# Transposing transfers of the SwiGLU product: issued by SyncE instead of ScalarE, later in SyncE's order, merged later, and in the second feed-forward only

## The chip, the cores and the metric

The kernel runs on one core of one Trainium2 chip. The metric is the device time of one execution in microseconds (us); a comparison takes the median of several runs. The core has these engines, by the names that the profile uses: PE (TensorE, matmuls and transposes through the array), DVE (VectorE), ACT (ScalarE), POOL (GpSimd) and SP (SyncE, which here only issues transfers). Transfers are carried out by 16 DMA engines; SP and ACT each have a queue of their own to them (q1 and q10 in the profile).

## The reference

One decoder layer on 256 positions of width 2048, in float32: a feed-forward, a pair of token mixers (retention and sliding-window attention) and a second feed-forward, each behind an RMS norm that is scaled and shifted by a conditioning vector, and a final norm. The change is in the feed-forwards:

```
def swiglu(h, w_gu, w_down):
    gate, up = jnp.split(h @ w_gu, 2, axis=-1)
    return (jax.nn.silu(gate) * up) @ w_down

x = x + 0.5 * mod[:, 2] * swiglu(h, w_ffn1_gu, w_ffn1_down)   # the first
...
x = x + 0.5 * mod[:, 8] * swiglu(h, w_ffn2_gu, w_ffn2_down)   # the second
return rms_norm(x, norm_final)
```

The inner width is 5632. The conditioning values mod are products of silu(c) with a weight matrix of 18432 rows.

## The kernel before

**Matmuls.** The 256 positions are two token tiles of 128. Every product is worked out in two parts for precision: weights and activations are each split into a high part (rounded to fp32r) and a low part, and three matmuls are made for each piece (L327 high x high, L328 low activation x high weight, L329 high activation x low weight). Weights come in tiles of 512 rows by 512 columns, 1 MB, into `raw`, a ring of four buffers (RAWS = 4) (`load`, L310). `split` (L331) makes of each half tile (256 rows) a high part wh by a cast on ACT (L335) and a low part wl by a subtraction on DVE (L336); each has a ring of three buffers. A half tile feeds 12 matmuls. A raw buffer is free for the next load when wl of its second half is done. `gemm` (L384) does one column block of 512: four tiles in the feed-forward's first product, with two PSUM banks of a ring of four.

**A feed-forward.** The inner width is 11 column blocks (ci = 0 to 10). For each, `ffn_up` (L585) makes the gate's product and the up product (8 weight tiles), and `swiglu_up` (L559) makes silu(gate) on ACT (L572) and times up on DVE (L573), for each token tile, into a tile s of 128 x 512 floats. The second product contracts over the inner width, so s is needed turned, inner width on the partitions. There are two ways to turn it:

- `transpose_to` (L413): four PE transposes of 128 x 128 (L417) into a PSUM bank and one copy back to SBUF (L418). The first six blocks of the first feed-forward, which are made in another loop (the groups of its beginning), and the last block of both use it.
- `turn_by_dma` (L424): transposing transfers move 2-byte words, so a float is taken apart. The function `apart` copies the low and the high words into two planes on ACT (L432) and issues a transposing transfer for each plane on ACT's queue (L433); `together` merges the two turned planes into the destination (L439), on an engine that is left open (`nc.any`, ACT or DVE). It has two buffers (tag "a"), one for each token tile of a block.

Blocks 6 to 9 of the first feed-forward and 0 to 9 of the second go the second way: 14 blocks, 28 tiles, 56 transfers.

**What sets the order.** SP's instructions stand in the order of the program. Those of PE, DVE and ACT are put in an order, at build time, by a planner that runs the program on a model of the chip and takes what the model says can start; on the chip each engine then takes its instructions strictly in that order. Within the program, `gemm` calls `step` (L300) after each weight tile, which advances the next piece of waiting side work by one. `later` (L549) is the side work of a block: `apart` of the two token tiles is called in the second and third step of the block behind, `together` in the fifth and sixth. Beside all this, `conditioning` (L241) loads rows of the conditioning weights (L199) and sums them on DVE (L204), at a set pace; in the second feed-forward these rows take buffers of the same ring `raw`, one after about every fifth weight tile.

## Time and profile before

| what | value |
|---|---|
| median of 3 runs | 2452.04 us |
| the runs | 2444.63, 2452.04, 2461.02 us |
| the profiled execution, its time | 2453.29 us |
| its span (first to last instruction) | 2451.4 us |
| TensorE clock granted in it, mean | 0.996 |
| transfers that transpose | 56, on ACT's queue |
| second feed-forward, its column blocks, in the span | about 1737 to 2203 us |

The profile is of one execution. Times in its rows are in us unless marked ns. A row of the waits gives the waiting engine and line, who ended the wait, the total, the number and the longest. A row of the stretches gives, for each engine, its busy time and in brackets the number of its instructions, then the granted clock of PE, the mean busy share of the 16 DMA engines and what they moved. A row of the timeline gives start, length, engine, line, operation, destination and sources, and in square brackets how long the engine was idle before and what ended that. Matmuls overlap in the records: one lasts 0.39 us there, but in a row of them one starts every 0.23. ACTq and SPq are the engines' issuing of transfers. A few per cent of matmul records can be missing.

### The profile page before, as it was taken

Reading aid. Unit: us, or ns where it says so; the run is one execution under the profiler, and the core shown is the slowest. Engines: PE = TensorE matmul, PEld = TensorE weight load, DVE = VectorE, ACT = ScalarE, POOL = GpSimd, SP = SyncE. Lnnn points to the kernel's source line nnn. Section 1 sums busy time; section 2 is a strip of 40 time slices with the busy share of each in tenths; the row PEclk is TensorE's granted clock in tenths of the full one; section 3 lists DMA queues with packets and bytes.
Section 4 is the critical chain, followed back from the end, with each engine's and each line's share of the span. In section 5 each row is a group of like instructions: output and inputs, shape, how many; then the busy total and the mean of one; then the engine's idle time right before and its main releaser. Section 6 shows DMA issues by size and latency. Waiting matters only on the chain. (4 is left out here: it accounts for less than half of the span.)

```text
span 2451.4 us, 29087 instructions
## 1 busy us (share of the span) xinstructions
PE 2393.8 (98%) x10798; PEld 1950.0 (80%) x10798; DVE 1711.5 (70%) x2767; ACT 1216.2 (50%) x1664; POOL 5.6 (0%) x14
## 2 busy tenths in 40 slices
PE   6999999999999999999999999999999999999998
PEld 4778888788787777788888888887788788888886
DVE  6998777678877677886666776767655556555656
ACT  6544544454445455554444444455544444444544
POOL 0000000000000000000000000000000000000000
PEclk9999999999999999999999999999999999999999
DMA  9897689998775655566677777754777667765563
GB/s 349 335 336 276 225 313 328 292 324 318 294 266 197 234 206 212 206 213 219 234 267 247 252 256 267 276 189 172 230 237 242 219 239 246 260 219 192 188 200 121
DMA packets 274545, 606.43 MB, mean 247 GB/s; under 512 B 40097, under 2 KB 40481, under 8 KB 255585
## 3 DMA queue, kind: packets, MB, share of 16 engines
q1 hardware_dynamic: 242434, 590.56, 68.0%
q10 hardware_dynamic: 31040, 8.40, 2.3%
q0 software_dynamic: 928, 5.61, 0.6%
q8 instruction: 85, 1.39, 0.2%
q14 instruction: 58, 0.48, 0.1%
HBM read 595.06 MB, written 2.12 MB: 244 GB/s over the span
## 5 line engine op out<-in xcount | busy, mean ns | idle before, releaser
L336 DVE TENSOR_TENSOR wl<-raw,wh 128x1024 fp32r<-128x1024 f32 (+1 forms) x828 | 994.1, 1206 | 580.7 <-ACT wh L335 577.3
L335 ACT CAST wh<-raw 128x1024 fp32r<-128x1024 f32 (+1 forms) x828 | 860.1, 1040 | 992.6 <-PE pa L328 952.2
L327 PE MATMUL pa<-wh,hh 128*128 128x512 f32 x2224 | 872.5, 393 | 8.6 <-ACT wh L335 8.0
L328 PE MATMUL pa<-wh,hl 128*128 128x512 f32 x2224 | 871.3, 392 | 2.3 <-DVE hl L500 1.8
L329 PE MATMUL pa<-wl,hh 128*128 128x512 f32 x2224 | 801.3, 393 | 11.3 <-DVE wl L336 11.0
L329 PEld LDWEIGHTS pa<-wl,hh 128*128 128x128 f32 x2224 | 416.5, 189 | 106.1 <-DVE wl L336 20.0
L327 PEld LDWEIGHTS pa<-wh,hh 128*128 128x128 f32 x2224 | 418.9, 189 | 100.1 <-ACT wh L335 10.6
L328 PEld LDWEIGHTS pa<-wh,hl 128*128 128x128 f32 x2224 | 419.1, 188 | 90.4 <-DVE hl L500 2.5
L328 PE MATMUL pa<-wh,a 128*128 128x512 f32 x992 | 384.4, 390 | 0.0
L327 PE MATMUL pa<-wh,a 128*128 128x512 f32 x992 | 367.7, 390 | 1.3 <-DVE t L543 1.2
L329 PE MATMUL pa<-wl,a 128*128 128x512 f32 x992 | 367.7, 391 | 0.8 <-DVE wl L336 0.8
L327 PEld LDWEIGHTS pa<-wh,a 128*128 128x128 f32 x992 | 186.6, 188 | 41.3 <-DVE t L543 1.9
L329 PEld LDWEIGHTS pa<-wl,a 128*128 128x128 f32 x992 | 186.4, 188 | 40.5 <-DVE wl L336 2.2
L328 PEld LDWEIGHTS pa<-wh,a 128*128 128x128 f32 x992 | 186.5, 188 | 38.6
L204 DVE CUSTOM_DVE_ANT_0 slot<-slot,cact 128x512 f32<-128x512 f32 (+1 forms) x252 | 192.9, 812 | 9.4 <-DMA slot<-in_w_ada_dram 9.2
L204 DVE CUSTOM_DVE_ANT_0 raw<-raw,cact 128x512 f32<-128x512 f32 (+1 forms) x260 | 166.9, 694 | 38.2 <-DMA raw<-in_w_ada_dram 27.6
L368 DVE TENSOR_TENSOR a<-slot,a 128x512 fp32r<-128x512 f32 x124 | 84.8, 684 | 14.8 <-ACT a L367 14.8
L367 ACT CAST a<-slot 128x512 fp32r<-128x512 f32 x124 | 76.6, 618 | 15.1 <-PE pa L329 14.7
L204 DVE DVE_READ_ACCUMULATOR2_ANT sums<- 128x1 f32 x512 | 41.7, 81 | 0.0
L418 ACT COPY slot<-ps 128x512 f32<-128x512 f32 x52 | 29.5, 584 | 23.7 <-PE ps L417 23.5
L459 ACT ACTIVATE pd<-x_sb 128x512 f32<-128x512 f32 x32 | 19.0, 593 | 35.2 <-DVE x_sb L544 32.5
L439 ACT COPY slot<-a 128x512 uint16<-128x512 uint16 x22 | 16.5, 770 | 39.2 <-DMA a<-a 39.1
(164 smaller groups left out, 1037.0 us busy)
## 6 DMA issues: line engine op xcount, KB each, us to landing
raw<-in_w_ffn_gu_dram SPq DMA_DIRECT2D x152, 1024.0 KB, 5.1
raw<-in_w_in_dram SPq DMA_DIRECT2D x104, 1024.0 KB, 5.0
raw<-in_w_ffn_down_dram SPq DMA_DIRECT2D x88, 1024.0 KB, 5.1
slot<-in_w_ada_dram SPq DMA_DIRECT2D x76, 1024.0 KB, 7.3
raw<-in_w_ada_dram SPq DMA_DIRECT2D x64, 1024.0 KB, 4.8
raw<-in_w_ffn_gu_dram SPq DMA_DIRECT2D x24, 768.0 KB, 6.5
raw<-in_w_swa_branch_dram SPq DMA_DIRECT2D x16, 1024.0 KB, 5.0
raw<-in_w_ret_branch_dram SPq DMA_DIRECT2D x16, 1024.0 KB, 5.1
```

Source lines behind the costliest of these rows:

```text
L204: nc.vector.tensor_tensor_reduce(out=w[:, at], in0=w[:, at], in1=cact[:, at], scale=1.0, scalar=0.0, op0=ALU.mult, op1=ALU.add, accum_out= ...
L327: nc.tensor.matmul(ps, ah[:, j, ts], wh[:, j, :], start=first, stop=False)
L328: nc.tensor.matmul(ps, al[:, j, ts], wh[:, j, :], start=False, stop=False)
L329: nc.tensor.matmul(ps, ah[:, j, ts], wl[:, j, :], start=False, stop=last)
L335: nc.scalar.copy(hi, src)
L336: nc.vector.tensor_sub(lo, src, hi.bitcast(F32))
L367: nc.scalar.copy(hi, v)
L368: nc.vector.tensor_sub(lo, v, hi.bitcast(F32))
L418: nc.any.tensor_copy(dest, ps[:, : n * P])
L439: nc.any.tensor_copy(into[:, :, :, i], turned[:, i])
L459: nc.scalar.activation(side_bank(), src, AF.Square, accum_out=dest)
```

## The change

Three things change in the code.

- Taking apart and issuing are separated. `apart` only makes the two word copies on ACT; a new function `turn` issues the two transposing transfers, on SP's queue instead of ACT's. Since SP keeps the program's order, the place where `turn` is called is its place among the weight loads.
- `later` has a new schedule: the word copies in the second and third step, as before; `turn` of the two token tiles in the seventh and eighth; the merging copies of both tiles in the step behind these, the first of the next block but one.
- `ffn_up` gets the set of column blocks that go by transfer. The call of the first feed-forward gives none, so its blocks 6 to 9 are turned by PE; the call of the second gives blocks 0 to 9, as before.

```
-                nc.scalar.dma_start_transpose(turned[:, i], planes[:, i, :])
+
+        def turn():
+            for i in range(2):
+                nc.sync.dma_start_transpose(turned[:, i], planes[:, i, :])
...
-        return apart, together
+        return apart, turn, together
...
     def later(work):
 
-        for first, _ in work:
+        (a0, t0, m0), (a1, t1, m1) = work
+        for f in (a0, a1, None, None, None, t0, t1, m0):
             yield
-            first()
-        yield
-        for _, second in work:
-            yield
-            second()
+            if f is not None:
+                f()
+        m1()
...
-    def ffn_up(held, w, tiles, first, bg=None):
+    def ffn_up(held, w, tiles, first, bg=None, turned=()):
...
-            swiglu_up(bg, bu, tiles, ci, by_dma=ci < DFF // CH - 1)
+            swiglu_up(bg, bu, tiles, ci, by_dma=ci in turned)
...
-    ffn_up(held, w_ffn2_gu[0], tiles, 0, head)
+    ffn_up(held, w_ffn2_gu[0], tiles, 0, head, range(DFF // CH - 1))
```

In the changed file the lines are a few further down: the transfers are L436, the merging copies L442, silu is L574.

The order on SP, in the second feed-forward, from the load of the last gate tile of column block 1 to the first gate tile of block 2. raw is the ring of weight tiles, a_2421 and a_2423 are the buffers in which the two token tiles of column block 0 are turned. Before:

```order
L312 DMA raw_2441_13692<-in_w_ffn2_gu_dram 128x4x512
L312 DMA raw_2448_13729<-in_w_ffn2_gu_dram 128x4x512
L199 DMA raw_2453_13763<-in_w_ada_dram 128x2048
L312 DMA raw_2454_13768<-in_w_ffn2_gu_dram 128x4x512
L312 DMA raw_2459_13805<-in_w_ffn2_gu_dram 128x4x512
L312 DMA raw_2464_13839<-in_w_ffn2_gu_dram 128x4x512
L312 DMA raw_2475_13884<-in_w_ffn2_gu_dram 128x4x512
```

The same place after the change:

```order
L312 DMA raw_2441_13680<-in_w_ffn2_gu_dram 128x4x512
L312 DMA raw_2448_13717<-in_w_ffn2_gu_dram 128x4x512
L199 DMA raw_2453_13751<-in_w_ada_dram 128x2048
L312 DMA raw_2454_13754<-in_w_ffn2_gu_dram 128x4x512
L312 DMA raw_2459_13789<-in_w_ffn2_gu_dram 128x4x512
L436 DMA_TRANSPOSE a_2421_13565<-a_2421_13565 128x4x128 x2
L312 DMA raw_2464_13825<-in_w_ffn2_gu_dram 128x4x512
L436 DMA_TRANSPOSE a_2423_13569<-a_2423_13569 128x4x128 x2
L312 DMA raw_2475_13872<-in_w_ffn2_gu_dram 128x4x512
```

Four transfers have come in, a pair behind each of two loads. The load raw_2459 goes into the buffer of raw_2441, four back in the ring, and raw_2464 into that of raw_2448.

The order on ACT at the turning of the same column block 0. wh is the high part of a half weight tile, t the tile s, slot the destination. Before, from the word copies to the merges (the other two merges of this block are on DVE):

```order
L432 COPY a_2421_13573<-t_2420_13570 128x512 x2
L432 COPY a_2423_13577<-t_2422_13574 128x512 x2
L433 DMA_TRANSPOSE a_2421_13573<-a_2421_13573 128x4x128
L335 CAST wh_2434_13633<-raw_2431_13615 128x1024
L433 DMA_TRANSPOSE a_2421_13573<-a_2421_13573 128x4x128
L433 DMA_TRANSPOSE a_2423_13577<-a_2423_13577 128x4x128
L335 CAST wh_2437_13655<-raw_2436_13653 128x1024
L433 DMA_TRANSPOSE a_2423_13577<-a_2423_13577 128x4x128
L335 CAST wh_2439_13672<-raw_2436_13653 128x1024
L439 COPY slot_2392_13421<-a_2423_13577 128x4x128
```

After the change the word copies stand at the same place, and the rest of this moves behind the cast wh_2449:

```order
L335 CAST wh_2444_13699<-raw_2441_13680 128x1024
L335 CAST wh_2449_13719<-raw_2448_13717 128x1024
L442 COPY slot_2392_13413<-a_2421_13565 128x4x128 x2
L335 CAST wh_2451_13735<-raw_2448_13717 128x1024
L574 ACTIVATE t_2469_13862<-pa_2424_13570 128x512
L335 CAST wh_2455_13756<-raw_2454_13754 128x1024
L574 ACTIVATE t_2471_13866<-pa_2425_13571 128x512
L442 COPY slot_2392_13413<-a_2423_13569 128x4x128 x2
L335 CAST wh_2457_13772<-raw_2454_13754 128x1024
```

The merges of a_2421 stand one cast behind the cast wh_2444, with whose half tile the buffer of raw_2441 comes free; those of a_2423 one cast (wh_2455) behind wh_2451, with which that of raw_2448 comes free. All four are on ACT here.

The order on ACT at column block 1, whose buffers are a_2470 and a_2472. On SP its first pair of transfers stands behind a load into the buffer of raw_2491, its second behind one into that of raw_2498. Before, around the word copies and the merge that is on ACT:

```order
L432 COPY a_2470_13877<-t_2469_13874 128x512 x2
L432 COPY a_2472_13881<-t_2471_13878 128x512 x2
L433 DMA_TRANSPOSE a_2470_13877<-a_2470_13877 128x4x128
L335 CAST wh_2483_13937<-raw_2480_13919 128x1024
L433 DMA_TRANSPOSE a_2470_13877<-a_2470_13877 128x4x128
L433 DMA_TRANSPOSE a_2472_13881<-a_2472_13881 128x4x128
L335 CAST wh_2487_13962<-raw_2486_13960 128x1024
L433 DMA_TRANSPOSE a_2472_13881<-a_2472_13881 128x4x128
L335 CAST wh_2489_13978<-raw_2486_13960 128x1024
L439 COPY slot_2392_13421<-a_2472_13881 128x4x128
```

After:

```order
L335 CAST wh_2494_14005<-raw_2491_13987 128x1024
L335 CAST wh_2499_14025<-raw_2498_14023 128x1024
L335 CAST wh_2501_14042<-raw_2498_14023 128x1024
L442 COPY slot_2392_13413<-a_2470_13865 128x4x128 x2
L574 ACTIVATE t_2519_14169<-pa_2473_13870 128x512
L335 CAST wh_2504_14060<-raw_2503_14058 128x1024
L574 ACTIVATE t_2521_14173<-pa_2474_13871 128x512
L335 CAST wh_2506_14077<-raw_2503_14058 128x1024
L442 COPY slot_2392_13413<-a_2472_13869 128x4x128 x2
L335 CAST wh_2509_14095<-raw_2508_14093 128x1024
```

Here the merges stand two casts behind the cast with whose half tile the buffer comes free (wh_2494 and wh_2501), not one. Counted in the same way over the ten blocks, it is one cast at blocks 0 and 5 for both token tiles and at 2 and 7 for the first, and two or more at the others.

## The prediction, made blind

> **What bounds the kernel now.** I read the page first: the share of each engine, the waits, the DMA queues.
>
> ```profile
> span 2451.4 us, 29087 instructions
> PE 2393.8 (98%) x10798; PEld 1950.0 (80%) x10798; DVE 1711.5 (70%) x2767; ACT 1216.2 (50%) x1664; POOL 5.6 (0%) x14
> q1 hardware_dynamic: 242434, 590.56, 68.0%
> q10 hardware_dynamic: 31040, 8.40, 2.3%
> ACT slot L439 <- DMA a<-a: 39.1, 17, 4.7
> DVE slot L439 <- DMA a<-a: 28.6, 13, 5.0
> ```
>
> TensorE (PE) is the bound: 98% busy. So an edit on ACT, DVE or SP is worth only the PE time that it frees or costs. The last two rows (the waits) name what this change touches: the merging copies (L439) stand waiting for a transposing transfer 30 times, 67.7 us in all. What matters is how much of that reaches PE. For this I took stretches of 20 us around each place where PE stood still beside a transfer, and two undisturbed ones (400 and 2000):
>
> ```profile
> core 0: us, PE busy (x) PEld busy (x) DVE busy (x) ACT busy (x) POOL busy (x), PEclk, DMA share, GB/s
> 360.00:380.00 20.00, 18.67 (x83) 15.14 (x82) 14.61 (x31) 9.81 (x12) 0.00 (x0) 1.00 0.91 299
> 460.00:480.00 20.00, 15.22 (x57) 11.11 (x57) 10.11 (x21) 8.97 (x11) 0.00 (x0) 0.91 0.89 227
> 400.00:420.00 20.00, 20.00 (x89) 16.54 (x89) 16.16 (x30) 10.39 (x13) 0.00 (x0) 1.00 0.99 324
> 1758.00:1778.00 20.00, 18.44 (x82) 14.92 (x81) 11.49 (x18) 8.35 (x9) 0.00 (x0) 1.00 0.82 230
> 1850.00:1870.00 20.00, 19.51 (x85) 15.50 (x85) 11.14 (x12) 8.92 (x11) 0.00 (x0) 1.00 0.77 269
> 1937.00:1957.00 20.00, 16.26 (x61) 12.92 (x61) 6.75 (x8) 7.70 (x8) 0.00 (x0) 0.83 0.76 184
> 2026.00:2046.00 20.00, 19.53 (x87) 15.85 (x86) 9.73 (x12) 9.06 (x11) 0.00 (x0) 1.00 0.79 221
> 2000.00:2020.00 20.00, 20.00 (x90) 16.57 (x89) 10.52 (x14) 8.84 (x10) 0.00 (x0) 1.00 0.52 178
> ```
>
> An undisturbed stretch holds 89.5 matmuls, 0.2235 us each. Those missing elsewhere, times this: first feed-forward 6.5 and 32.5, so 1.5 + 7.3 = 8.8 us; second 7.5, 4.5, 28.5 and 2.5, so 1.7 + 1.0 + 6.4 + 0.6 = 9.7 us. Everything that the transposing transfers cost PE is 18.5 us, 0.75% of the span. That caps the gain.
>
> The timeline of the costliest stop in the second feed-forward shows how it comes about:
>
> ```profile
> 1936.01 1.29 ACTq L433 DMA_TRANSPOSE a<-a  x1
> ...
> 1942.03 0.39 PE L328 MATMUL pa<-wh,hl 128*128 128x512 f32 x1
> 1944.54 0.45 DVE L439 COPY slot<-a 128x512 uint16<-128x512 uint16 x1 [4.40 <-DMA a<-a]
> 1944.89 3.48 DVE L336 TENSOR_TENSOR wl<-raw,wh 128x1024 fp32r<-128x1024 f32 x3
> ...
> 1946.16 1.22 PE L329 MATMUL pa<-wl,hh 128*128 128x512 f32 x2 [3.74 <-DVE wl L336]
> 1947.18 0.63 PE L327 MATMUL pa<-wh,hh 128*128 128x512 f32 x1
> 1947.61 0.63 PE L328 MATMUL pa<-wh,hl 128*128 128x512 f32 x1
> ...
> 1951.83 0.40 PE L327 MATMUL pa<-wh,hh 128*128 128x512 f32 x1
> 1952.06 0.39 PE L328 MATMUL pa<-wh,hl 128*128 128x512 f32 x1
> ```
>
> DVE sits in front of a merging copy, behind which the low part of the weights (wl) is queued; PE wants wl and stands 3.74 us. Afterwards its matmuls start 0.43 us apart instead of 0.23 for some 5 us. Of the 6.4 us, 3.9 are the stop (1942.03 to 1946.16, less one matmul) and 2.5 the slow restart. The 1.56 us idle of the 1758 row left the clock (PEclk) at 1.00, the 3.74 here took it to 0.83.
>
> **The change, part by part.**
>
> *First feed-forward: four column blocks go back to PE transposes.* Gone: 16 transfers with their copies, hence the stops of 8.8 us. Added: 8 transposes in each block. Priced by the last block, which does this already, in the chain of waits:
>
> ```profile
> 2203.62 0.87 PE ps L417 x8
> ```
>
> 4 x 0.87 = 3.5 us, all on PE. Their evacuations (two copies a block) replace eight word copies a block, off the path. A wait of PE for the product that it transposes would cost extra; that last block shows none, I take 0, at most 1 us a block. Net -5.3 us (-5.3 to -1.3).
>
> *Second feed-forward: ACT loses 40 issues, SP gains them.* It frees up to 4 x 1.25 us of ACT a block, at a place where its casts wait for PE anyway (1.67 us before each, rows below): 0, since PE is never waiting for ACT there. On SP four issues of about 1.2 us a block (1.21 to 1.29 in the rows quoted) stand ahead of weight loads. A load has three weight tiles of 5.44 us each (two halves of 2.72, below) before it is wanted, 16.3 us, and lands in 5.1 us (row below), so 2.5 us per pair is covered; without that cover each pair would cost up to 2.5 us of PE. The transfers wait for ACT's word copies, with the weight loads queued behind; these copies stand eight casts, some 21 us, ahead of the merges, so SP doesn't wait: 0. The later merges hold the two buffers of `turn_by_dma` longer; the next word copies come 13 casts behind: 0. POOL's queue is not touched.
>
> *Where the merges now stand.* The code calls them at the ninth step, but ACT and DVE are ordered by the planner, and it pulls them forward, right behind the issues. The cadence of one half tile, in rows of the timeline (the last one is the SP queue's, its later loads merged into it):
>
> ```profile
> 1925.00 1.05 ACT L335 CAST wh<-raw 128x1024 fp32r<-128x1024 f32 x1 [1.67 <-PE pa L328]
> 1927.72 1.05 ACT L335 CAST wh<-raw 128x1024 fp32r<-128x1024 f32 x1 [1.67 <-PE pa L328]
> 1927.75 0.39 PE L327 MATMUL pa<-wh,hh 128*128 128x512 f32 x1
> 1928.65 0.62 PE L329 MATMUL pa<-wl,hh 128*128 128x512 f32 x2
> 1928.81 1.23 DVE L336 TENSOR_TENSOR wl<-raw,wh 128x1024 fp32r<-128x1024 f32 x1 [1.50 <-ACT wh L335]
> 1930.06 17.57 SPq L312 DMA_DIRECT2D raw<-in_w_ffn_gu_dram  x4
> ```
>
> A cast every 2.72 us; its wl is done 2.32 us after it starts; SP's next load leaves at 2.34. There are three wh buffers, so a cast runs two halves ahead of its matmuls, which want wl 0.9 us after they start: a cast may be 2 x 2.72 + 0.9 - 2.34 = 4.0 us late before PE stops.
>
> Column block 0, with C the start of the cast wh_2444 (the rows of ACT and SP are in the section on the change). SP passes the load raw_2459 when raw_2441 is free: T = C + 2.34. Directly behind it the first tile's two transfers. ACT has one cast in between (wh_2449) and is at the merges at C + 3.77. When do the transfers land? Two transfers of before left within 0.3 us behind a load (rows of the SP and ACT timelines: the load, the transfer, the merge that waited for it):
>
> ```profile
> 1804.17 0.37 SPq L312 DMA_DIRECT2D raw<-in_w_ffn_gu_dram  x1
> 1804.44 1.20 ACTq L433 DMA_TRANSPOSE a<-a  x1
> 1810.34 0.77 ACT L439 COPY slot<-a 128x512 uint16<-128x512 uint16 x1 [2.31 <-DMA a<-a]
> 2160.74 0.37 SPq L312 DMA_DIRECT2D raw<-in_w_ffn_gu_dram  x1
> 2160.95 1.21 ACTq L433 DMA_TRANSPOSE a<-a  x1
> 2166.39 0.77 ACT L439 COPY slot<-a 128x512 uint16<-128x512 uint16 x1 [1.80 <-DMA a<-a]
> raw<-in_w_ffn_gu_dram SPq DMA_DIRECT2D x152, 1024.0 KB, 5.1
> ```
>
> 6.2 and 5.65 us after the load's issue: 5.9. From below, the load itself (5.1) bounds it. The second plane comes behind the first: q10's 2.3% of 2451.4 us over 56 transfers is 1.0 us each; the 0.45 us between DVE's landing at 1944.54 and ACT's next merge is less; I take 0.7. So T + 5.9 and T + 6.6, that is C + 8.24 and C + 8.94. A pair of merges ends 0.76 after the second landing (one takes 0.77): C + 9.7. The next cast was due at C + 5.44: 4.26 late, 0.26 past the slack. From it hangs everything of the second tile: wl ends and the load raw_2464 leaves at C + 12.04, the transfers land at C + 17.94 and 18.64, their merges end at C + 19.4. Only one cast stands ahead of them, the next (wh_2457) was due at C + 10.88 + 0.26: 8.26 late, 4.26 past the slack. A stop of about 4.3 us, plus the slow restart of 2.5, plus the 0.26: 7.0 us.
>
> In the changed order this place (one cast between release and merge, for both tiles) comes twice among the ten blocks, at 0 and 5, since the conditioning loads shift the ring of four; blocks 2 and 7 have it for the first tile, and their second tile's transfers leave right behind the first's, with a load between, so they land a few us later, when ACT is one cast further; I reckon one more cast's length past the slack, 0.26 + 1.05 = 1.3 us. The other six have two casts between: ACT arrives 2.72 us later, the cast behind is then 1.5 us late, inside the slack: 0. Sum 2 x 7.0 + 2 x 1.3 = 16.6 us against 9.7 now: +6.9.
>
> From below: landing at T + 5.1 and 5.5 makes the same steps end with the second cast 6.8 late, a stop of 2.8, between the 1.56 us idle that cost no restart and the 3.74 that did; I count none: 2 x 2.8 = 5.6 us, -4.1 against now (with restarts +0.9). From above: the longer landing, T + 6.2, and the second plane a whole issue (1.3 us) behind: stops of 1.2 + 5.2 and the restart, 8.9 twice, and 2 twice: 21.8 us, +12.1.
>
> [...]
>
> Sum: -5.3 + 6.9 = +1.6 us. The profiled execution took 2453.3 us (span 2451.4), the median of the three runs is 2452.0, so it stands 1.3 above; the sum against it gives 2454.9, on the median 2453.6. I say 2453.
>
> **The rivals.** About 1% (24.5 us) is what a measurement of this kernel can tell from no change.
>
> The spread of all 56 landings:
>
> ```profile
> DMA to landing us min/median/max: 2.4/4.9/20.9
> ```
>
> - *Transfers land with the load.* [...] For it: the fastest landing, 2.4 us, shows that a transfer by itself is short. Against: the two landings of 5.65 and 6.2.
> - *The first feed-forward doesn't gain.* Its stop at 462 may come from loads that are late there anyway (DMA share 0.89 to 0.99 in its rows, against 0.52 at 2000); then only 1.5 us go, 3.5 come: +2.0 + 6.9 = +8.9, 2461. Against: merging copies stood for up to 5.0 us (the waits above), more than the 4.0 us of slack worked out above, which is enough for such a stop.
> - *SP's queue is slow, and the kernel slower.* If SP's transfers land 3 us later than reckoned (T + 9), the steps above give 14 us at each of blocks 0 and 5 (stops of 3.4 and 7.4, a restart or two), about 6 at 2 and 7, and 1 at the other six: 46 us, +36 against now, +31 in all: 2483. It passes 1% from about T + 8.5. For it: landings reach 20.9 us. Against: the DMA engines have room in the second feed-forward, share 0.52 to 0.82 in its stretches.
> - *The late merging that the code writes is not what runs.* That is part of the forecast already: the planner undoes it.
>
> **How the numbers follow.** Forecast 0.58 (2443 to 2463 by its bounds: -5.3 - 4.1 to -1.3 + 12.1), landing with the load 0.22, no gain in the first feed-forward 0.10, slow queue 0.08, something unseen 0.02. The range 2440 to 2468 takes the first three, with a few microseconds for runs that lay from 2444.6 to 2461.0. Faster by over 1% would need more than the 18.5 us there are: 0.03, for what I don't see. Slower by over 1% is the slow queue and a bit: 0.09. Within 1%: 0.88.
>
> **What would show it.** The stops of 360 and 460 gone, and 32 more transposes in the L417 group on t. In the second feed-forward, ACT's waits in front of merges longer than now (about 4.5 us each at blocks 0, 2, 5, 7, about 1.7 elsewhere), a stop of about 4 us with a slow restart at each of blocks 0 and 5, none as long elsewhere. Wrong if landings of SP's transfers are not 5.5 to 7 us behind their load, if weight loads come late for casts, or if PE stops at the new transposes.

## The result, and the profile after the change

The changed kernel takes 2435.14 us (median of 6 runs, 2434.28 to 2438.25), the kernel before beside it 2454.68 us (6 runs, 2444.63 to 2465.43): a ratio of 0.9922, 95% interval 0.9893 to 0.9951. On another chip it was 2435.93 against 2457.70 us, 0.9911 (0.9887 to 0.9935). So it is some 20 us, 0.8%, faster. That is inside the 1% that was forecast, but 5 us below the low end of the range, and on the other side of "before" than the sum of terms said (+1.6 us). The runs also lie closer together: 4 us apart, where those of before are 21 us apart.

The page of the changed kernel, its lines that answer to those shown of before:

```profile
span 2433.4 us, 29081 instructions
PE 2390.0 (98%) x10830; PEld 1949.4 (80%) x10830; DVE 1701.0 (70%) x2735; ACT 1222.5 (50%) x1672; POOL 5.7 (0%) x14
q1 hardware_dynamic: 264194, 595.81, 69.8%
q10 hardware_dynamic: 576, 1.05, 0.1%
```

The profiled execution took 2435.17 us, and its span is 18.0 us shorter than that of before. PE has 32 more instructions (the transposes of four blocks) and yet is busy for 3.8 us less; its idle time, span less busy, fell from 57.6 to 43.4 us. The transfers have moved from q10 to q1: q10 has 7.35 MB less, 131 KB for each of the 56, which is 128 x 512 words of two bytes. The waits in front of the merging copies:

```profile
ACT slot L442 <- DMA a<-a: 28.7, 16, 3.5
...
DVE slot L442 <- DMA a<-a: 1.5, 2, 0.7
```

ACT and DVE still stand there 18 times for 30.2 us, the longest for 3.5 (before: 30 times, 67.7 us, 5.0). What came of it on PE is in the stretches, taken around the longest stops of before, at the first one of the second feed-forward (1757) and once where there was none (2000):

```profile
core 0: us, PE busy (x) PEld busy (x) DVE busy (x) ACT busy (x) POOL busy (x), PEclk, DMA share, GB/s
459.00:479.00 20.00, 20.00 (x90) 16.58 (x89) 15.25 (x28) 9.34 (x10) 0.00 (x0) 1.00 0.95 364
...
1757.00:1777.00 20.00, 20.00 (x90) 16.57 (x89) 10.43 (x15) 11.72 (x14) 0.00 (x0) 1.00 0.88 288
1935.00:1955.00 20.00, 20.00 (x90) 16.57 (x89) 11.98 (x16) 10.77 (x13) 0.00 (x0) 1.00 0.86 239
2000.00:2020.00 20.00, 20.00 (x90) 16.58 (x89) 13.16 (x18) 9.41 (x12) 0.00 (x0) 1.00 0.65 227
```

Every one is full: 90 matmuls, clock 1.00. In the whole of the second feed-forward the waits of PE have no row any more; from 340 to 620 us one of 0.3 us is left. Before, they were these (first the stretch of the first feed-forward's last blocks, 340 to 620 us, then the second feed-forward, 1737 to 2203 us):

```profile
PE pa L327 <- ACT wh L335: 4.7, 2, 3.2
PE pa L329 <- DVE wl L336: 1.3, 1, 1.3
...
PE pa L329 <- DVE wl L336: 5.8, 3, 3.7
PE pa L327 <- ACT wh L335: 0.4, 1, 0.4
```

Of the 18.0 us, the prediction's own count of the stops (18.5 with their restarts) less 3.5 us of transposes gives 15.0. The starts of the same matmuls in the two traces say 14.6: 4.5 from 340 to 620 us, 10.1 in the second feed-forward. The rest lies at places without a transfer, mostly from 20 to 40 and 650 to 670 us, which differ between executions of before as well.

### Column block 0 of the second feed-forward, where the prediction expected a stop of 4.3 us

The timeline of the changed kernel, rows of SP, ACT and DVE (the conditioning's sums are L204):

```profile
1756.52 2.82 SPq L312 DMA_DIRECT2D raw<-in_w_ffn_gu_dram  x2
...
1758.24 0.69 DVE L204 CUSTOM_DVE_ANT_0 raw<-raw,cact 128x512 f32<-128x512 f32 x1
1758.86 0.08 DVE L204 DVE_READ_ACCUMULATOR2_ANT sums<- 128x1 f32 x1
...
1759.39 2.61 SPq L436 DMA_TRANSPOSE a<-a  x2
1759.62 1.06 ACT L335 CAST wh<-raw 128x1024 fp32r<-128x1024 f32 x1 [1.66 <-PE pa L328]
1760.71 1.23 DVE L336 TENSOR_TENSOR wl<-raw,wh 128x1024 fp32r<-128x1024 f32 x1 [0.63 <-ACT wh L335]
1762.10 0.53 SPq L312 DMA_DIRECT2D raw<-in_w_ffn_gu_dram  x1
1762.34 1.06 ACT L335 CAST wh<-raw 128x1024 fp32r<-128x1024 f32 x1 [1.66 <-PE pa L328]
...
1764.78 1.40 ACT L442 COPY slot<-a 128x512 uint16<-128x512 uint16 x2 [1.39 <-DMA a<-a]
1766.05 1.04 ACT L335 CAST wh<-raw 128x1024 fp32r<-128x1024 f32 x1
...
1769.25 1.40 ACT L442 COPY slot<-a 128x512 uint16<-128x512 uint16 x2
```

The cast wh_2444 is the one at 1759.62: that is C. The load raw_2459 is the second of the two in the first row; that row ends at 1759.34 and an issue takes 0.37, so it left at 1758.97. That is C - 0.65, where the prediction had T = C + 2.34. It left 0.03 us after the last sum on the conditioning row (1758.86 + 0.08) and 3 us before wl of raw_2441 was done (1760.71 + 1.23 = 1761.94). So it went into the buffer of the conditioning row, not of raw_2441, as the section on the change said. The buffer of raw_2441 is then left for the load after it (raw_2464), which left at 1762.10. The ring of four doesn't turn strictly: a conditioning row gives its buffer back early, and the next load takes it.

The rest of the first tile's step came as reckoned. The transfers landed at 1764.76, 5.8 us behind the load's issue (T + 5.9 was said); two merges took 1.27; the next cast started at 1766.05, 1.0 us late instead of 4.3, and no stop followed. The second tile, from which the prediction's stop of 4.3 us came, was early too: its load left at C + 2.5 instead of C + 12.0, and its merges (1769.25) did not wait at all.

Not every block is like this one. The time from issue to landing, over the 40 transfers of the changed kernel:

```profile
DMA to landing us min/median/max: 4.4/5.5/9.1
```

The first tile's transfers landed 5.8 to 6.4 us behind the load (or the conditioning row) ahead of them at eight of the ten blocks, but 8.7 and 9.5 us behind it at blocks 2 and 7, where two other loads had left within 3.5 us before; four second tiles were over 7 us as well. That is outside the 5.5 to 7 us that the prediction named. No stop came of it: at blocks 2 and 7 three casts start between the load and the merge, not two as at the other eight, and ACT waited for 1.9 and 2.8 us.

### The profile page after: what moved, and what is told of

It reads as the page before. It is cut to its first block, busy times and chain, and to the rows that moved or that the text cites. A ratio compares the mean times of both kernels' runs of the same rounds, so it can differ in the third digit from the quotient of the medians.

```text
span 2433.4 us, 29081 instructions
## 1 busy us (share of the span) xinstructions
PE 2390.0 (98%) x10830; PEld 1949.4 (80%) x10830; DVE 1701.0 (70%) x2735; ACT 1222.5 (50%) x1672; POOL 5.7 (0%) x14
## 3 DMA queue, kind: packets, MB, share of 16 engines
q8 instruction: 85, 1.39, 0.2%
## 5 line engine op out<-in xcount | busy, mean ns | idle before, releaser
L327 PE MATMUL pa<-wh,hh 128*128 128x512 f32 x2224 | 870.3, 393 | 3.4 <-ACT wh L335 2.9
L328 PE MATMUL pa<-wh,hl 128*128 128x512 f32 x2224 | 870.1, 391 | 2.2 <-DVE hl L503 1.7
L329 PE MATMUL pa<-wl,hh 128*128 128x512 f32 x2224 | 798.9, 392 | 4.0 <-DVE wl L336 3.9
L327 PEld LDWEIGHTS pa<-wh,hh 128*128 128x128 f32 x2224 | 418.0, 188 | 93.4 <-ACT wh L335 4.3
L329 PEld LDWEIGHTS pa<-wl,hh 128*128 128x128 f32 x2224 | 415.5, 188 | 95.7 <-DVE wl L336 9.8
L328 PEld LDWEIGHTS pa<-wh,hl 128*128 128x128 f32 x2224 | 418.3, 188 | 89.4 <-DVE hl L503 2.4
L328 PE MATMUL pa<-wh,a 128*128 128x512 f32 x992 | 383.8, 389 | 0.0
L329 PE MATMUL pa<-wl,a 128*128 128x512 f32 x992 | 367.6, 390 | 1.4 <-DVE wl L336 1.4
L327 PE MATMUL pa<-wh,a 128*128 128x512 f32 x992 | 367.2, 390 | 0.3 <-DVE t L546 0.2
L329 PEld LDWEIGHTS pa<-wl,a 128*128 128x128 f32 x992 | 185.6, 188 | 42.4 <-DVE wl L336 4.5
L327 PEld LDWEIGHTS pa<-wh,a 128*128 128x128 f32 x992 | 186.1, 188 | 40.6 <-DVE t L546 0.9
L328 PEld LDWEIGHTS pa<-wh,a 128*128 128x128 f32 x992 | 186.2, 188 | 38.5
L204 DVE CUSTOM_DVE_ANT_0 slot<-slot,cact 128x512 f32<-128x512 f32 (+1 forms) x252 | 192.9, 815 | 23.9 <-DMA slot<-in_w_ada_dram 23.8
L204 DVE CUSTOM_DVE_ANT_0 raw<-raw,cact 128x512 f32<-128x512 f32 (+1 forms) x260 | 167.1, 696 | 38.5 <-DMA raw<-in_w_ada_dram 28.0
L204 DVE DVE_READ_ACCUMULATOR2_ANT sums<- 128x1 f32 x512 | 42.7, 83 | 0.0
L442 ACT COPY slot<-a 128x512 uint16<-128x512 uint16 x38 | 26.8, 769 | 28.8 <-DMA a<-a 28.7
```

The source lines that it names most:

```text
L204: nc.vector.tensor_tensor_reduce(out=w[:, at], in0=w[:, at], in1=cact[:, at], scale=1.0, scalar=0.0, op0=ALU.mult, op1=ALU.add, accum_out= ...
L327: nc.tensor.matmul(ps, ah[:, j, ts], wh[:, j, :], start=first, stop=False)
L328: nc.tensor.matmul(ps, al[:, j, ts], wh[:, j, :], start=False, stop=False)
L329: nc.tensor.matmul(ps, ah[:, j, ts], wl[:, j, :], start=False, stop=last)
L442: nc.any.tensor_copy(into[:, :, :, i], turned[:, i])
```

## The experiments

The times are medians in us:

| run | first feed-forward, blocks 6 to 9 | second, blocks 0 to 9 | time (range) | ratio to before on the same chip |
|---|---|---|---|---|
| before | ACT's queue, early | ACT's queue, early | 2454.7 to 2463.2 on five occasions | 1 |
| the change | PE | SP, late | 2435.14 (2434.28 to 2438.25) | 0.9922 |
| the change again | PE | SP, late | 2435.93 (2435.37 to 2436.37) | 0.9911 |
| first only | PE | ACT's queue, early | 2440.66 (2439.49 to 2441.86) | 0.9930 (0.9914 to 0.9946) |
| second only | ACT's queue, early | SP, late | 2450.74 (2442.43 to 2452.36) | 0.9968 (0.9952 to 0.9985) |
| no transfers | PE | PE | 2445.43 (2443.99 to 2445.86) | 0.9948 (0.9929 to 0.9967) |
| both by SP | SP, late | SP, late | 2431.79 (2431.47 to 2432.05) | 0.9893 (0.9878 to 0.9909) |
| SP early | PE | SP, early | 2440.62 (2439.76 to 2442.07) | 0.9930 (0.9914 to 0.9946) |
| both SP early | SP, early | SP, early | 2449.85 (2447.39 to 2451.22) | 0.9956 (0.9940 to 0.9973) |
| one step later | PE | SP, one load later | 2434.98 (2434.61 to 2436.86) | 0.9909 (0.9885 to 0.9933) |
| rows early | PE | SP, late | 2436.06 (2434.86 to 2437.05) | 0.9913 (0.9883 to 0.9942) |
| late on ACT | ACT's queue, late | ACT's queue, late | 2438.12 (2436.82 to 2452.32) | 0.9930 (0.9905 to 0.9954) |

"First only", "both by SP", "SP early" and "no transfers" ran on one chip; "the change again", "second only", "one step later" and "rows early" on another; "both SP early" and "late on ACT" on one more each. The ratio takes in all runs of both kernels, so it is not exactly the quotient of the two medians. Where two versions from different chips are compared below, a difference of a microsecond says little: the change itself was 2435.1 on one and 2435.9 on the other.

### The parts of the change, one at a time

The change again, as the base on the second chip:

> The changed kernel itself, on the same chip as the three others. Both theories: 2434 to 2439 us, runs within some 4 us of each other; it is the base of the comparisons.

2435.93 us, runs 1 us apart.

First only: the schedule and the queue of before, without the blocks of the first feed-forward.

```
-            swiglu_up(bg, bu, tiles, ci, by_dma=ci < DFF // CH - 1)
+            swiglu_up(bg, bu, tiles, ci, by_dma=ci in turned)
...
-    ffn_up(held, w_ffn2_gu[0], tiles, 0, head)
+    ffn_up(held, w_ffn2_gu[0], tiles, 0, head, range(DFF // CH - 1))
```

> The kernel before with one part of the change alone: the first feed-forward turned by PE, the second left as it was (transfers on ACT's queue, merges where they were). Theory A, the two halves add up: the stops of the first feed-forward (8.8 us) go and 3.5 us of PE transposes come, the second keeps its stops (9.7 us in the profile of before, more or less in another run): 5 us faster than before, and the spread from run to run of before, some 20 us, stays for the most part. Rival B, the first feed-forward is all there is: the whole 19 us, with the small spread of the changed kernel. Rival C, the stops there come from late loads and stay: 2 us slower.

17.8 us faster than before: not theory A's 5, nearly B's 19. In the second feed-forward one stop is left, here in the waits of PE from 1730 to 2196 us:

```profile
PE pa L329 <- DVE wl L336: 2.9, 1, 2.9
```

So not all of the 17.8 us belongs to the first feed-forward. By the starts of the matmuls this trace is 3.4 us shorter than the first trace of before from 340 to 620 us, and 5.4 us shorter in the second feed-forward, where it has one wait of PE in place of four although the code is that of before, and the order of ACT's and DVE's work too. Its merges wait for their transfers for less there (29.7 us in all, against 47.2); why is open.

Second only: the other half, the first feed-forward as before.

```
+        if not late:
+            for f in (lambda: a0(True), lambda: a1(True), None, m0, m1):
...
-    ffn_up(held, gu, tiles, EARLY)
+    ffn_up(held, gu, tiles, EARLY, None, range(DFF // CH - 1))
+    late.append(1)
```

> The second feed-forward as after the change, blocks 6 to 9 of the first as before it (issued by ACT in the second and third step, merged in the fifth and sixth). Theory A, both halves of the change bring something: the second feed-forward has no stops at its transfers, the first has those of before (9.0 us in the one trace) and not the 3.5 us of transposes, so after + 5.5 us, 2441, and more (up to 2455) if these stops are longer in other runs than in the traced one; and the runs lie as far apart as those of before (some 10 to 20 us), since it is these stops that vary. Rival B, the gain belongs to the first feed-forward alone: no faster than before, 2452 to 2460. Rival C, the gain belongs to the second alone: 2432, after - 3.5, runs close together.

2450.74 us, 14.8 above the change again on the same chip and 7.0 below before, with runs 10 us apart: theory A. B would have been before's time, C a time below the change's. Its waits of PE from 340 to 620 us (L330 and L328 are L329 and L327 here):

```profile
PE pa L330 <- DVE wl L337: 4.5, 1, 4.5
PE pa L328 <- ACT wh L336: 4.0, 1, 4.0
```

This is one of its shorter executions (2444.36 us). In the second feed-forward it has no wait of PE, as after the change. This run and the change again differ in the first feed-forward alone, so its part is worth 14.8 us of the median, and the second's the 7.0 that are left to before. Taken the other way round, by "first only", it is 17.8 and some 5, but there part of the second feed-forward's gain is in the 17.8.

Two more traced executions of the kernel before are to show what makes its runs differ.

> The kernel before, one more execution with its trace, to see what differs between its executions (2444 to 2465 us so far). Theory A: the stops at the transposing transfers of the first feed-forward differ, in place and size (9.0 us in the first trace), everything else is the same within a microsecond or two. Rival B: the second feed-forward's stops differ. Rival C: the difference is spread over the whole span.

> As the look before, another execution: the span less that of the first trace (2451.4 us) should be the difference of the stops of 340 to 520 us by theory A, of those of 1737 to 2203 us by B.

The spans were 2446.6 and 2456.3 us, against 2451.4 in the first trace. The waits of PE from 340 to 620 us in the longest of the three:

```profile
PE pa L327 <- ACT wh L335: 5.7, 3, 2.7
PE pa L329 <- DVE wl L336: 4.6, 1, 4.6
```

That is 10.3 us against 6.0 in the first trace (and 5.6 in the shortest), while the second feed-forward had 6.6, 6.2 and 6.1 us. So theory A holds for the longest: by the starts of the matmuls it is 8.0 us behind the first trace from 340 to 620 us (4.3 of them are these waits; it also has three slow restarts there against one, the granted clock at 0.91, 0.91 and 0.83 in 366 to 386, 466 to 486 and 418 to 428 us), and 3.1 us ahead of it elsewhere, which makes the 4.9. The 4.8 us between the first and the shortest are not there; they are spread over the beginning, the place around 660 us and the second feed-forward, 1.2 to 1.8 us in each.

No transfers: what PE's transposes cost.

```
-    ffn_up(held, w_ffn2_gu[0], tiles, 0, head, range(DFF // CH - 1))
+    ffn_up(held, w_ffn2_gu[0], tiles, 0, head)
```

> No transposing transfers at all: both feed-forwards turned by PE. Against the changed kernel ten more blocks of 8 transposes at 0.87 us come on PE: 8.7 us slower than the changed kernel if that has no stops left in the second feed-forward, as its profile says. If PE also had to wait for the products that it turns, more. If the changed kernel still loses something to its transfers that the profile does not show, less.

9.5 to 10.3 us above the change: ten blocks at 0.87 us are 8.7, and by the starts of the matmuls the second feed-forward is 9.1 longer, 0.91 a block. So the transfers of the changed kernel cost PE nothing that can be seen, and the price of the transposes is nearly right.

Both by SP: the first feed-forward's blocks by SP as well.

```
-    ffn_up(held, gu, tiles, EARLY)
+    ffn_up(held, gu, tiles, EARLY, None, range(DFF // CH - 1))
```

> The changed kernel with the transfers of SP, at the new places, in the first feed-forward as well (blocks 6 to 9), so without its PE transposes. Theory A, what stops PE is a merge that stands too soon behind a transfer of ACT's queue: the stops are gone here too and the 3.5 us of PE transposes with them, 3.5 us faster than the changed kernel. Rival D, the first feed-forward keeps the DMA engines busy (share 0.89 to 0.99), transfers land late whoever issues them: stops of 5 to 10 us come back there, 2 to 7 us slower than the changed kernel.

3.3 to 4.1 us below the change, about the 3.5 of the transposes, on another chip but with ranges that don't touch: the fastest version here, 1.07% below before. Its first feed-forward has no transposes on PE and no stops; by the starts of the matmuls it is 9.1 us shorter there than the first trace of before, where the prediction had counted 8.8 us of stops.

### Why the merges don't wait for long

Two runs bring back the prediction's T. In the first the transfers leave one load later and the merges are called right behind them:

```
-        for f in (a0, a1, None, None, None, t0, t1, m0):
+        for f in (a0, a1, None, None, None, None, t0, t1):
...
+        m0()
         m1()
```

> After the change, but the transfers one step (one weight load) later on SP, and the merging copies called right behind them. At column block 0 the first pair then leaves behind the load into the buffer of raw_2441, that is at C + 2.5, as the prediction had it for the change itself. Theory A, the planner knows when the load leaves and moves the merges with it, so that ACT waits only for what a transfer takes longer on the chip than the planner reckons (1 to 3.5 us now), inside the 4.0 us of slack: no stop, as after within 2 us. Rival B, the prediction's step (a merge stands so and so many casts behind the release, whatever the planner knows): stops of about 4 us with a slow restart at two blocks or more, 7 to 20 us slower than after.

2434.98 us, as the change; no wait of PE in the second feed-forward, ACT's longest at a merge 3.3 us. Theory A. At block 0 the load ahead of the first pair left at C + 2.34 (1762.10), and in the planner's order the first merge now stands behind wh_2451, a cast further back; it didn't wait.

In the second the conditioning rows are done with in the first half of the second feed-forward, and the ring turns strictly after that:

```
-    set_pace([(8, None, 0.5)], 160, raw_row, 2)
+    set_pace([(8, None, 0.5)], 80, raw_row, 2)
```

> After the change, but the conditioning rows of the second feed-forward are paced over 80 half tiles instead of 160, so that they share the ring of weight buffers in its first half only. Behind that the ring turns strictly over four buffers, and the load ahead of a pair leaves 2.3 to 2.5 us behind the start of the cast with which its buffer comes free, the prediction's T = C + 2.34, at all blocks of the second half. Theory A: ACT's waits in front of merges stay at 1 to 3.5 us there, no stops: as after within 3 us (denser rows in the first half may cost a little). Rival B, with the release that late the merges are late too: stops of 4 us and more at some of the blocks 5 to 9, 7 to 30 us slower than after.

2436.06 us, as the change again (2435.93). The timeline in the strict half:

```profile
1971.99 1.05 ACT L335 CAST wh<-raw 128x1024 fp32r<-128x1024 f32 x1 [1.62 <-PE pa L328]
...
1974.33 0.37 SPq L312 DMA_DIRECT2D raw<-in_w_ffn_gu_dram  x1
1974.71 1.05 ACT L335 CAST wh<-raw 128x1024 fp32r<-128x1024 f32 x1 [1.67 <-PE pa L328]
1974.75 2.68 SPq L436 DMA_TRANSPOSE a<-a  x2
...
1977.43 1.05 ACT L335 CAST wh<-raw 128x1024 fp32r<-128x1024 f32 x1 [1.67 <-PE pa L328]
...
1980.10 1.40 ACT L442 COPY slot<-a 128x512 uint16<-128x512 uint16 x2 [1.62 <-DMA a<-a]
1981.37 1.03 ACT L335 CAST wh<-raw 128x1024 fp32r<-128x1024 f32 x1
```

Here T is C + 2.34 to the hundredth (1974.33 less 1971.99), the transfers land 5.8 us later (1980.10, when ACT's wait ends), as the prediction reckoned, and yet ACT waits 1.62 us and the next cast is 1.2 us late: two casts stand between release and merge, not one. ACT comes to the merge at 1980.10 - 1.62 = 1978.48, 4.15 us behind the load; in the changed kernel at 1764.78 - 1.39 = 1763.39, 4.4 behind its load. The same holds for both tiles of all five blocks in the strict half: two casts, ACT 4.15 to 4.17 us behind the load, a wait of 1.6 to 1.9 us. In the changed kernel ACT never comes sooner: 4.15 to 4.4 us at the first tiles of eight blocks, later at the other two and at most second tiles. That fits a planner that knows when the load can leave and sets the merge by that, so that ACT waits only for what the chip takes longer than the planner reckoned; the planner's own times are not on record, so this much is argued. The case of the prediction, T at C + 2.34 and one cast in between, occurs nowhere in the changed kernel: at the first tiles of blocks 0 and 5, where the prediction counted one cast, the load left right behind a conditioning row's sums. Where something like it does occur, at four second tiles of these two runs, ACT came 2.7 to 3.6 us behind the load, not the 1.4 of the prediction, and its waits of 2.3 to 3.1 us stopped nothing.

The slack of 4.0 us that the prediction worked out for a cast is not contradicted by the longest wait of the changed kernel:

```profile
1944.58 1.06 ACT L335 CAST wh<-raw 128x1024 fp32r<-128x1024 f32 x1 [1.14 <-PE pa L328]
...
1949.13 1.41 ACT L442 COPY slot<-a 128x512 uint16<-128x512 uint16 x2 [3.50 <-DMA a<-a]
...
1950.40 1.99 ACT L335 CAST wh<-raw 128x1024 fp32r<-128x1024 f32 x2
```

The cast at 1950.40 was due at 1947.30 (1944.58 + 2.72). It is 3.1 us late, and PE has no wait there, so the slack is at least that. (The transfers had a conditioning row in front, and landed 7.2 us behind their issue; why later than others is open.)

### SP's queue, its place, and ACT's queue

SP early: the transfers on SP's queue, but called where before had them.

```
-        for f in (a0, a1, None, None, None, t0, t1, m0):
+        for fs in ((a0, t0), (a1, t1), (), (m0,), (m1,)):
             yield
-            if f is not None:
+            for f in fs:
                 f()
-        m1()
```

> The changed kernel with SP issuing the transfers directly behind the word copies in the program (steps 2 and 3, merges called in steps 5 and 6, as before the change), so SP's queue without the later place. Theory E, the queue is what helps: as the changed kernel within 3 us. Theory F, the later place is what helps, since SP in its order now has to wait for ACT's word copies while weight loads stand behind: SP waits on ACT some 10 to 20 us a block, loads leave late, PE waits for casts, 10 to 40 us slower than the changed kernel.

5.5 us above the change (2435.14; 4.7 above the change again), between the theories, both of which it misses: F's direction, not its size. The cause is F's. The waits of SP and then of ACT in its second feed-forward (from 1730 us):

```profile
SPq L436 <- ACT a L432: 153.4, 10, 19.1
...
ACT wh L335 <- DMA raw<-in_w_ffn_gu_dram: 52.7, 25, 4.6
```

SP stands in front of a transfer until the word copy is made, 15 us a block, with weight loads queued behind; the loads come late, and ACT's casts wait for them. By the starts of the matmuls the second feed-forward is 6.4 us longer than after the change, though the waits of PE there are only one of 1.5 us: most of the delay is spread over many matmuls. This is the wait that the prediction looked at and put at nothing for the late place. It is nothing there and about 5 us here.

Both SP early has this in both feed-forwards; on top of the edit of SP early:

```
-    ffn_up(held, gu, tiles, EARLY)
+    ffn_up(held, gu, tiles, EARLY, None, range(DFF // CH - 1))
```

> Both feed-forwards by transfers as in the kernel before, in its place in the program (issued at the second and third step, merged at the fifth and sixth), but on SP's queue instead of ACT's. Theory A, it is the queue that makes landings long in the first feed-forward (a transfer on ACT's queue shares the engines with whatever SP's queue has outstanding, 9 us median and up to 21; on SP's own it comes behind the load just issued): landings of at most 11 us there, no stop over 3 us at 360 to 480, the runs within 4 us of each other; the weight loads queued behind cost what they cost in the run that had this only in the second feed-forward, so that run - 3.5 us or a few more: 2437 to 2443. Rival B, the place in time makes it (loads and conditioning rows are dense there): landings up to 15 to 20 us as before, stops of 9 to 20 us, 2446 to 2460, runs 10 us and more apart.

2449.85 us, outside what theory A gave and inside B's range, though for another reason than B's: the landings are short (2.4 to 7.7 us in the first feed-forward), and PE's waits from 340 to 620 us are six of at most 1.0 us (4.2 in all), behind casts that waited for late loads (49.2 us from 340 to 520 us). Since SP issues no loads while it stands in front of a transfer (154.1 us at the ten blocks of this run's second feed-forward), this doesn't tell queue from place. The last run keeps the place: both by SP, but each pair issued on ACT's queue, pinned behind the cast that runs about when SP issued it.

```
-        nc.scalar.copy(hi, src)
+        casts.append(nc.scalar.copy(hi, src))
...
-            for i in range(2):
-                nc.sync.dma_start_transpose(turned[:, i], planes[:, i, :])
+            with tc.issue_after(casts[-7].ins):
+                for i in range(2):
+                    nc.scalar.dma_start_transpose(turned[:, i], planes[:, i, :])
```

> The run with both feed-forwards turned by transfers late in SP's order (2431.8 us, landings of 5.3 to 10.8 us in the first feed-forward, the second plane some 0.5 us behind the first, no stops), but the transfers issued on ACT's queue, each pair right behind the cast of wh that runs about when SP issued them, so at the same place in time. The merges stand where the planner puts them. Theory A, the queue makes the long landings: beside a busy SP queue a pair of transfers on a queue of its own takes 3 to 6 us each instead of 0.5, landings reach 12 to 21 us in the first feed-forward, ACT waits over 4.4 us at some merges, PE stops there: 2440 to 2460, the runs 5 us and more apart. Rival B, the early place in time made them long: landings as with SP's queue, at most 11 us; four issues of about 1.25 us a block on ACT stay within the slack: 2431 to 2436, runs within 4 us.

2438.12 us, with five runs from 2436.8 to 2439.1 and two at 2451.0 and 2452.3. The time from issue to landing, minimum, median and maximum, of the 16 transfers of the first feed-forward; in the kernel before:

```profile
DMA to landing us min/median/max: 3.2/6.6/20.9
```

In "both by SP", where PE has no wait from 340 to 620 us:

```profile
DMA to landing us min/median/max: 5.3/7.8/10.8
```

In "late on ACT", and its waits of PE there:

```profile
DMA to landing us min/median/max: 2.9/7.2/11.4
...
PE pa L329 <- DVE wl L338: 3.1, 2, 2.8
PE pa L327 <- ACT wh L337: 0.6, 1, 0.6
```

The stop of 2.8 us (at 452.88 us) is not at a transfer. DVE, behind whose work the wl that PE wants was queued, stood in front of the sums on a conditioning row:

```profile
449.15 0.69 DVE L204 CUSTOM_DVE_ANT_0 slot<-slot,cact 128x512 f32<-128x512 f32 x1 [4.57 <-DMA slot<-in_w_ada_dram]
```

Why that row landed so late is open. What a merge cost PE in this trace is the 0.6 us. So in the traced execution theory B holds for the landings, though not for its time of 2431 to 2436: with the late place on ACT's queue the longest landing is 11.4 us, against 20.9 in the first trace of before, and SP's queue at that place has hardly shorter ones (10.8). In the second feed-forward the place is enough: here too PE has no wait, and by the starts of the matmuls it is 10.1 us shorter than the first trace of before, as much as after the change. What the place doesn't explain is two of seven runs that are 13 us longer (A's spread); these weren't traced, and whether the queue makes them is open. What can be said is that a transfer on ACT's queue landed anywhere from 2.4 to 20.9 us behind its issue in the first trace of before (the prediction's spread of all 56) and from 2.5 to 11.4 in "late on ACT", and that on SP's queue, late, it was 4.4 to 9.1 us in the changed kernel and 5.3 to 10.8 in the first feed-forward of "both by SP", and the runs of each of the two lie within 4 us of each other.

## Why the prediction was wrong

**The step that failed** is the term of the second feed-forward, +6.9 us (stops of 16.6 us after, 9.7 now), and in it the sentence "SP passes the load raw_2459 when raw_2441 is free: T = C + 2.34". The load left at C - 0.65, into another buffer. Behind it stood a wrong way of reading: the casts between release and merge were counted from the order of the changed kernel, and the release was put in from a rule of the ring, as if the order had been made without it. The runs fit a planner that makes both from the same times: "rows early" shows that with T at C + 2.34 the order has one cast more. The term is -9.7: no stop is left, and the starts of the matmuls give -10.1.

**The term of the first feed-forward** (-5.3 us) is right for the traced execution: its 8.8 us of stops are gone and 3.5 us of transposes have come ("both by SP" shows the first, 9.1 by the starts of the matmuls, and "no transfers" the price of the second). For the median it was too small: "second only" puts it at 14.8 us. The stops were sized by one execution that had 6.0 us of waits there, where the longest traced one had 10.3 and was 8.0 us longer in that stretch. The cap of 18.5 us was a cap on that execution; the median fell by 19.5. The spread of the runs of before, 16 us in the three shown, stood beside it and was used for the range only.

**The lower end** (-4.1 us, and with it 2443) counted no slow restart behind stops of 2.8 us and 0.4 us from the first plane's landing to the second's. No run shows the first for a stop at a merge: in the longest trace of before one of 2.65 us, in "first only" one of 2.86 us was followed by the slow pace (last section). The second was the author's estimate; the changed kernel has 0.41 to 0.66 us.

**What held.** The landing: T + 5.9 said, 5.8 measured at block 0 and 5.8 to 6.4 at eight of ten blocks, though 8.7 and 9.5 at the other two, which the prediction named as a sign of being wrong. In the changed kernel the second plane landed 0.41 to 0.66 us behind the first, less than the 0.7 that was taken. The slack of 4.0 us: a cast 3.1 us late stopped nothing. SP's four issues a block and the wait for the word copies at nothing: in the second feed-forward of the changed kernel ACT never waits for a weight load in front of a cast. (The word copies stand four to seven casts ahead of the first merges, 17.8 us at block 0, not eight casts and 21 us; the term is nothing all the same.) No stop at the new transposes. The rival "transfers land with the load" came closest in time (landings at T + 5.1 are those of the lower end, 2443), but not by its mechanism. That the time stays within 1% came true as well, but by a gain of 0.8% and not by a sum near nothing.

**What would show it.** The stops of 360 and 460 gone, and 32 more transposes: yes. Waits of 4.5 us at blocks 0, 2, 5 and 7: no, 1.4, 1.9, 2.0 and 2.8 us for the first tile, and at most 3.5 anywhere. About 1.7 elsewhere: yes, 1.7 to 1.9. A stop at blocks 0 and 5: none. Landings of 5.5 to 7 us behind their load: not always, as said.

## What to carry to other kernels

Where a planner sets the order, don't join a position from its order with a time from a rule of your own: the order already holds the planner's times, and what remains to be priced is by how much the chip's transfer lands later than its consumer's place allows for (here mostly 1.4 to 2 us, up to 3.5). Here a transfer issued late, when its source was ready, with its consumer placed behind it by the planner, stopped PE little or not at all in the traced executions, on either queue (no wait of PE in the changed kernel's second feed-forward or in "both by SP", 0.6 us at a merge in "late on ACT"); issued early on SP's queue, it held up the loads behind it (in "SP early" SP stood for 15 us a block, and the kernel took 5 us longer). And a cap on a gain has to be taken from several executions when the kernel's runs differ by more than the change is about.

## What the runs showed of the hardware that was not expected

The slow restart came after shorter stops than the prediction's lower end assumed, which counted none at 2.8 us. PE in "first only":

```profile
1932.74 0.39 PE L328 MATMUL pa<-wh,hl 128*128 128x512 f32 x1
1935.99 1.22 PE L329 MATMUL pa<-wl,hh 128*128 128x512 f32 x2 [2.86 <-DVE wl L336]
1937.01 0.63 PE L327 MATMUL pa<-wh,hh 128*128 128x512 f32 x1
1937.43 0.63 PE L328 MATMUL pa<-wh,hl 128*128 128x512 f32 x1
```

After 2.86 us idle the matmuls start 0.42 us apart instead of 0.23, until 1939.1. In "late on ACT" the stop of nearly the same length behind the conditioning row is followed by the full pace at once:

```profile
449.74 0.39 PE L328 MATMUL pa<-wh,hl 128*128 128x512 f32 x1
452.88 0.73 PE L329 MATMUL pa<-wl,hh 128*128 128x512 f32 x2 [2.76 <-DVE wl L338]
453.45 0.40 PE L327 MATMUL pa<-wh,hh 128*128 128x512 f32 x1
453.69 0.40 PE L328 MATMUL pa<-wh,hl 128*128 128x512 f32 x1
```

In the first and the longest trace of before, "first only", "second only" and "late on ACT" there are ten stops of 2.65 us or more in the stretches of the transfers: nine at a merge, and this one. In the 10 or 20 us around each of the nine the granted clock was 0.83 to 0.91; behind those of 2.65, 2.86 and 3.74 us the slow pace lasted some 3 to 5 us. This one was followed by none, and the stops of 1.33 and 1.56 us in the first trace of before left the clock at 1.00. Stops of 2.65 and 2.86 us were followed by the slow pace and one of 2.76 us was not, so the recorded length alone doesn't decide it here, and 2.65 us can be enough. The lower end of the prediction, with stops of 2.8 us at a merge, should have been the +0.9 that it named beside it.
